# A hybrid decoder step with 32 experts: weight loads moved ahead of the read of a branch count, one more weight buffer, and the PSUM sums taken over 15 of 16 pairs

## The chip, the cores and the metric

The kernel runs on one core of one Trainium2 chip. The metric is the device time of one execution in microseconds. The kernel before was timed in three runs; the trace that is read below comes from one more, profiled execution. Engines are named as in the profile: PE is TensorE (PEld its weight loads), DVE VectorE, ACT ScalarE, POOL GpSimd, SP SyncE, which here only issues transfers.

## The reference, cut to what matters

One decoder layer is applied to 256 prompt tokens and to 8 x 8 sample tokens, 320 tokens in all, of width 1024. An adaLN projection of the conditioning gives shifts, scales and gates (`g1`, `g2`). A mixer follows (chunked gMLP and a gated linear recurrence), its output projection `w_out`, and a layer norm. Then comes the part that takes most of the time, the mixture of experts with a hidden width of 512:

```
lg = x2 @ w_rg + b_rg                       # 4 groups, top 1
le = (x2 @ w_re + b_re) of the chosen group # 8 experts, top 2
for each of the 32 experts e:
    hdn = silu(x2 @ w1[e]) * (x2 @ w3[e])   # 1024 -> 512
    acc = acc + gate[:, e] * (hdn @ w2[e])  # 512 -> 1024
x = layer_norm(ALPHA * x + (1 + g2) * acc, ln2_g, ln2_b)
```

`w1`, `w3` and `w2` have 2 MB for each expert and are read in float32: 192 MB in all. Only the tokens routed to an expert need its product.

## The kernel before, in words

**Weight buffers.** Big tiles come from two rings of 8 KB per partition (L42, `SLOTS = (8, 8)`): `slot(name, i=0)` and `slot(name, i=1)`. A ring hands on the buffer that was released first, and a tile is released after its last use in the code. The first ring holds in turn `ini`, `md` and `gx` (long-lived scratch), the adaLN weights `wada`, the halves of `w_in` and `w_out` (`wq`) and every even expert load; the second one holds the split `w_in` parts, the two `mb` tiles, `pd` and every odd expert load.

**Expert loads.** Each expert's `w1`, `w3` and `w2` come as six loads of 1 MB (tile `we`, L636). They go out on SP's queue in one fixed order: both up-projections of a pair of experts, then the down-projections of the pair before. `load_until(n)` issues them up to the n-th:

```
PIECES = [(e, i, h) for e, some in ORDER for i, h in some]
...
for e, i, h in PIECES[pieces:n]:
    w = slot("we", (128, kk, 2048 // kk), i=pieces % 2)
```

Loads 0 to 3 are issued at L639, in front of the last adaLN weights (L640) and the output projection (`out_proj`, L647). Loads up to 14 (`AHEAD = 15`) are issued at L895, and from there each pair p begins with `load_until(20 + 12 * p)` (L1137). A load waits in SP's queue for its buffer; whatever is behind it on SP waits too. At most eight transfers are under way, since each reuses the semaphore of the one eight before it.

**Routing.** `out_proj` and `norm` run over the three token tiles (128, 128 and 64 tokens); `turn_h2` (L689) transposes the normalised tokens, `logits` (L699) multiplies them with the router weights, `route` picks group and experts, `count` and `arrange` give every token its place, and `sort` (L851) gathers the tokens in order of expert into `xD`. Tiles of the pools `ab` and `mid` end here, and `xD` takes their space.

**The branch.** Each expert handles up to 24, 24 and 16 tokens of the three tiles in the main path. If some expert has more, an extra loop runs (`more_rounds`, L1010), which loads its own weights in 512-column chunks (tile `ck`, L1028, in the ring of tag `s` together with the silu tile of `swish`, L963). All engines read the count into a register:

```
n_most = nc.values_load(most[0:1, 0:1], min_val=0, max_val=NT, ...)     # L889
load_until(AHEAD)                                                      # L895
...
with tc.If(n_most > CAP):                                              # L1129
    gates_and_windows(); gates(); more_rounds()
```

With these inputs the branch is not taken. At the join, the semaphores that the body would have raised are made up for: SP waits until each of its eight transfer semaphores has reached the count of the loads issued so far, then adds what the body would have added. Consumers behind the join whose tile shares a ring with a tile of the body wait for those counts.

**Pairs of experts.** The main loop (L1136) goes over 16 pairs. `up_of(e)` (L1089) is the up-projection of one expert on PE (L959), followed by `swish` on ACT (L964) and DVE (L965); `turn_of` transposes the hidden rows of a pair (L971) and multiplies them with the gates (L974, `hT`); `downs(p - 1)` is the down-projection of the pair before (L983). Its two results are taken out of PSUM as a rounded part by ACT (L990) and the rest by DVE (L991). `places` (L946) builds the matrix that puts a pair's rows back to their tokens, and `combine` (L1000) adds them, both parts, into the five PSUM banks `pc` (L1004, L1008), which stay open over the pairs. That leaves three PSUM banks for all else.

**The last pairs.** `SUMMED = 14` pairs are summed so. After the 14th, `take()` (L1066) multiplies the sums by `g2` and adds them to the residual `xk` on DVE, and the last two pairs go another way: DVE multiplies their outputs by `g2k` when it takes them from PSUM (L987), `begin(t)` (L1044) puts the residual into the banks `pc` by an identity matmul (L1046), and `prompt_sum` and `sample_sum` (L1048, L1051) add the unsplit float32 rows. `begin_rest` (L1055) prepares the rows for the second layer norm, which ends the kernel. `g2k`, the broadcast `g2`, is a tile of its own in the pool `late`; `spread("g2", ...)` fills it at pair 2 with POOL and DVE (L511, L513).

Of the kernel before, what the change touches and what calls it, by code (L numbers as in the profile page):

```python
# [6 lines left out]
F32 = mybir.dt.float32  # L7
F32R = mybir.dt.float32r
BF16 = mybir.dt.bfloat16
# [13 lines left out]
XO = (0, 280, 560)  # L23
NP = 704
ROUNDS = 5
SUMMED = NE // 2 - 2
AHEAD = 15
SLOTS = (8, 8)
EPS = 1e-5
ALPHA = 2.0 ** 0.25  # L30
LRU_C = 8.0
# [6 lines left out]
def hymba_step(tc, I, O):  # L38
    nc = tc.nc
    with ExitStack() as ctx:  # L40
# [23 lines left out]
        eps = keep.tile([128, 1], F32, name="eps")  # L64
        mm = keep.tile([128, 2, 128], BF16, name="mm")
        before, ones = mm[:, 0, :], mm[:, 1, :]
        zz = keep.tile([1, 640], BF16, name="zz")
        zero, ones512 = zz[:, 0:128], zz[:, 128:640]
        io32 = keep.tile([128, 3, NE], F32, name="io32")
        io4 = keep.tile([128, 3, 4], F32, name="io4")  # L70
        one = keep.tile([128, 1], F32, name="one")
        lg = keep.tile([128, 3, 40], F32, name="lg")

# [46 lines left out]
        V.tensor_scalar(before, jp, 0.0, None, op0=OP.is_gt)  # L120
        V.memset(ones, 1.0)
        V.memset(zero, 0.0)
        V.memset(ones512, 1.0)
        V.memset(eps, EPS)
        V.memset(one, 1.0)
        V.memset(one[0:64], 0.0)
# [446 lines left out]
        proj_f(wy, yr_done, False, lambda: fill(2))  # L573
        early_.close()
        late = ctx.enter_context(tc.tile_pool(name="late", bufs=1, side="left"))
        g2k = late.tile([128, 2, D], F32, name="g2k")
        M = late.tile([128, 3, NE], BF16, name="M")
        sp1T = late.tile([NE, NT], F32R, name="sp1T")
        mod3 = late.tile([128, 256], F32, name="mod3")
        offs = late.tile([128, 3, NE], F32, name="offs")  # L580
        offi = late.tile([1, 3, NE], I32, name="offi")
        offf = late.tile([1, 3, NE], F32, name="offf")
        offr = late.tile([1, 3, NE], I32, name="offr")

        PT2 = [late.tile([128, 448], F32R, name=f"PT{i}") for i in range(2)]
# [1 line left out]
        h2 = scp.tile([128, 3, D], F32, name="h2")  # L587
        oh12 = scp.tile([128, 3, 2, NE], F32, name="oh12")
        io256 = late.tile([128, 256], F32, name="io256")
        mb["g2"] = (g2k[:, 0, :], g2k[0:64, 1, :])  # L590
        mb["sc2"] = (sck[:, 0, :], sck[0:64, 1, :])

        sc, sh, tmp = mod[:, 2, 0:256], mod[:, 1, 256:512], ini[:, 0:256]
# [31 lines left out]
        def load_until(n):  # L625

            nonlocal pieces
            for e, i, h in PIECES[pieces:n]:
                kk = (4, 4, 2)[i]
                w = slot("we", (128, kk, 2048 // kk), i=pieces % 2)  # L630
                pieces += 1
                src = (w1d, w3d, w2d)[i][e].rearrange("(p h k) n -> h p k n", h=2, k=kk)[h]
                parts = 2 if e == NE - 1 and i == 2 and h else 1
                step = kk // parts
                for c in range(0, kk, step):
                    nc.sync.dma_start(w[:, c:c + step], src[:, c:c + step])  # L636
                held[e, 2 * i + h] = w
# [1 line left out]
        load_until(4)  # L639
        w_g2 = load_ada2(3)  # L640
        V.memset(lg[64:128, 2, :], 0.0)
        h2T0 = mid.tile([128, D], F32, name="h2T0")
        h2T = {2: md_[:, 0:512], 0: h2T0, 1: mb["g1"][0]}
        h2T = {t: a.rearrange("p (k q) -> p k q", k=8) for t, a in h2T.items()}
        st1 = {}

        def out_proj(t, n2s=(0, 1)):  # L647
# [41 lines left out]
        def turn_h2(t, h):  # L689
            n = TW[t]  # L690
            p = bank("p2", (128, 4, 128))
            for k in range(4):
                kk = 4 * h + k
                T.transpose(p[:, k, :n], h2[:n, t, kk * 128:(kk + 1) * 128], ident[:n, :n])
            S.copy(h2T[t][:, 4 * h:4 * h + 4, :n], p[:, :, :n])

        pr = {}

        def logits(t, ks):  # L699
            n = TW[t]  # L700
            for k in ks:
                if k == 0:
                    pr[t] = bank("pr", (128, 40))
                T.matmul(pr[t][:n], h2T[t][:, k, :n], wr[:, k, :], start=(k == 0), stop=(k == 7))

        def logits_end(t):
            n = TW[t]
# [177 lines left out]
        for t in range(3):  # L885
            V.tensor_copy(offi[:, t, :], offs[0:1, t, :])
            ranks(t)
        V.tensor_reduce(most, over.rearrange("p t e -> p (t e)"), axis=AX.X, op=OP.max)
        n_most = nc.values_load(most[0:1, 0:1], min_val=0, max_val=NT,  # L889
                                skip_runtime_bounds_check_because="a count of the tokens")  # L890
        for t in range(3):
            W = XO[t] + WID[t]
            G.memset(xD[:, :, W:W + CAPS[t]], 0.0)
            G.memset(gD[:, W:W + CAPS[t]], 0.0)
        load_until(AHEAD)  # L895
        sorted_out(1)
        ada_end(3)

# [96 lines left out]
        pc = {(t, q): bank("pc") for t in range(2) for q in range(2)}  # L995
        pc[2] = bank("pc")
        for p in pc.values():
            T.matmul(p, zero, ones512, start=True, stop=False)

        def combine(yg, PT, stop=False):  # L1000
            for q in range(2):
# [7 lines left out]

        def more_rounds():  # L1010

            V.tensor_copy(offf, offs[0:1])
            with tc.For_i(0, ROUNDS, 1):
                for t in range(3):
                    V.tensor_scalar(rank[:, t, :], rank[:, t, :], -float(CAPS[t]), None, op0=OP.add)
                    V.tensor_scalar(offf[:, t, :], offf[:, t, :], float(CAPS[t]), float(WID[t]), op0=OP.add, op1=OP.min)
                    windows_of(t)
                V.tensor_copy(offr, offf)
                turn_places()
                with tc.For_i(0, NE, 2) as e:  # L1020
                    two = exs.tile([NE, 2], F32, name="two")
                    V.tensor_copy(two, ident[0:NE, bass.ds(e, 2)])
                    PT = places(select(two))
                    yg = [exs.tile([128, D], F32R, name=f"y{i}") for i in range(2)]
                    h = exs.tile([128, 512], F32, name="h")

                    def chunk(src, a, k, kk, cs):
                        c = exs.tile([128, 512], F32, name="ck", tag="s")  # L1028
                        v = src[bass.ds(e + a, 1)].rearrange("o (p k) n -> p (o k) n", k=kk)
                        nc.sync.dma_start(c, v[:, k, cs])  # L1030
                        return c

                    gT = exs.tile([128, 2, CAP], F32, name="gT")
                    for a in range(2):
                        xT, vs = window([offr[0:1, t, bass.ds(e + a, 1)] for t in range(3)], "xTm")
                        window_gates(gT, a, vs)
                        swish(a, up(lambda q, k: chunk((w1d, w3d)[q], a, k, 8, slice(0, 512)), xT), h)
                    hT = turn(h, gT)
                    for a in range(2):
                        down(a, lambda q, k: chunk(w2d, a, k, 4, slice(q * 512, q * 512 + 512)), hT, yg)  # L1040
                    combine(yg, PT)
# [93 lines left out]
        LAST = NE // 2 - 1  # L1135
        for p in range(NE // 2):  # L1136
            load_until(20 + 12 * p)  # L1137
            if p < LAST:
                select_of(p)
            if p == 0:  # L1140
                fetch(1)
                gates_and_windows()
            up_of(2 * p)
            fetch(2 * p + 2)
            if p == 2:
                spread("g2", 2, (range(4), slice(256, 512)))
            if p == 5:
                row1 = slot("row1", (1, 2048), i=1)
                G.dma_start(row1[:, 0:1024], I["ln1_g"])
                G.dma_start(row1[:, 1024:2048], I["ln1_b"])  # L1150
                ln1 = slot("ln1", (128, 2048))
                G.partition_broadcast(ln1, row1, channels=128)
            if 6 <= p < 9:
                whiten[p - 6]()
                residual(p - 6)
            if p >= 2 and p < LAST:
                combine(ys.pop(p - 2), PTs.pop(p - 2))
            if 0 < p < LAST:
                places_of(p)
            fetch(2 * p + 3)  # L1160
            if p == LAST:
                downs(p - 1)
                begin(0)
                begin(1)
                for t in range(2):
                    for q in range(2):
                        prompt_sum(t, q, ys[p - 1], PTs[p - 1], False)
                sample_sum(ys[p - 1], PTs[p - 1], False)
            second = up_of(2 * p + 1)
            if p == 0:  # L1170
                gates()
                gates_of(0, first)
                gates_of(1, second)
                turn_places()
                places_of(0)
            if p == LAST - 2:
                f1 = slot("f1", (128, 128), i=1)
                fold = f1.rearrange("p (a n) -> p a n", a=2)
                sv = exs.tile([128, 2], F32, name="sv")
                f2 = slot("f2")  # L1180
                g2s, G2s, B2s, xs = (f2[:, 512 * i:512 * i + 512] for i in range(4))
                lrow = slot("lrow", (1, 2048), i=1)
                G.dma_start(lrow[:, 0:1024], I["ln2_g"])  # L1183
                G.dma_start(lrow[:, 1024:2048], I["ln2_b"])
                lbc = slot("lbc", (128, 2048))
                G.partition_broadcast(lbc, lrow, channels=128)
            if p == LAST - 1:
                begin_rest()
            if p and p < LAST:
                downs(p - 1)  # L1190
            turn_of(p)
            if p == LAST - 1:
                combine(ys.pop(p - 1), PTs.pop(p - 1), True)
                select_of(LAST)
                places_of(LAST)
                take()
        S.activation(sv[:, 0:1], eps, AF.Sqrt)
        down_of(NE - 2)
        S.activation(sv[:, 0:1], eps, AF.Sqrt)
# [81 lines left out]
```

## Time and profile before

| | us |
|---|---|
| runs of the kernel before | 691.79, 687.49, 690.62 (median 690.62) |
| profiled execution, its own time | 687.08 |
| its span | 685.3 |
| PE busy (2762 matmuls) | 600.3 (88% of the span) |
| DVE busy | 276.0 (40%) |
| ACT busy | 127.9 (19%) |
| POOL busy | 51.7 (8%) |

HBM reads are 241.49 MB, 355 GB/s over the span. The own time is 1.8 us longer than the span, which begins with the first and ends with the last record of an engine.

The page cuts the span into 40 slices of 17.1 us. In the rows of groups and of the timeline stand: start or line, engine, operation, written tile <- read tiles, partitions x elements, count; what a bracket or the last column holds is the idle time of the engine just before and what ended it. In a row of waits the numbers are the total, the count of waits, and the longest. A row of windows gives, for a stretch, the busy time of PE, PEld, DVE, ACT and POOL with their counts, then the granted PE clock, the DMA share and GB/s. A PE that is busy need not be the bound: its matmuls are pipelined.

### The profile page before, as it was taken

What the parts mean: (1) busy time and instruction counts of PE and PEld (TensorE: products, weight loads), DVE (VectorE), ACT (ScalarE), POOL (GpSimd) and SP (SyncE); (2) the same over time, 40 slices, a digit from 0 to 9 for tenths busy, and PEclk for the clock granted to TensorE, in tenths of its full rate; (3) what the DMA queues carried; (4) which work ended last, traced back from release to release, by engine and by line L of the source; (5) the groups of instructions that cost most, each with busy time, mean ns of one, the idle gap of its engine ahead of it and who ended that gap; (6) DMA issues with size and microseconds to landing.
All of it is one profiled execution on the core that took longest, in us unless ns stands there. A gap on an engine that the chain in (4) does not pass through costs nothing.

```text
span 685.3 us, 7676 instructions
## 1 busy us (share of the span) xinstructions
PE 600.3 (88%) x2762; PEld 272.7 (40%) x2762; DVE 276.0 (40%) x748; ACT 127.9 (19%) x219; POOL 51.7 (8%) x81
## 2 busy tenths in 40 slices
PE   5599999999974999998989898897989989897982
PEld 1396688356621343332323333232332323233320
DVE  1399484966522243233134243322323132225226
ACT  0255651111201011111012111101111010112121
POOL 2031415300010000000020000000000000100002
PEclk9989999999795999999999999999999999998997
DMA  8997678831298999999999999999999999999902
GB/s 336 383 324 268 237 250 314 307 127 63 105 424 328 426 427 427 426 427 427 427 426 427 427 427 426 427 425 428 425 428 426 427 427 427 425 427 427 413 23 77
DMA packets 42493, 243.57 MB, mean 355 GB/s; under 512 B 5630, under 2 KB 6374, under 8 KB 15954
## 3 DMA queue, kind: packets, MB, share of 16 engines
q1 hardware_dynamic: 41650, 242.58, 86.9%
q0 software_dynamic: 800, 0.45, 0.3%
q8 instruction: 23, 0.38, 0.2%
q14 instruction: 20, 0.16, 0.1%
HBM read 241.49 MB, written 1.52 MB: 355 GB/s over the span
## 4 chain that ended last, share of the span: by engine, by line
DMA 46%; PE 18%; DVE 2%; ACT 1%; issue 0%; SPq 0%; ACTq 0%
DMA we<-in_w 46%; PE p L959 9%; PE p L983 5%; PE pc L1004 1%; PE pc L1049 1%; PE pc L1008 1%; PE pc L1046 1%; PE ph L971 0%; DVE y L991 0%; PE pc L1053 0%; PE pr L949 0%; PE pgd L909 0%; DVE xk L1249 0%; DVE h L965 0%; DVE f L987 0%
## 5 line engine op out<-in xcount | busy, mean ns | idle before, releaser
L959 PE MATMUL p<-we,xT 128*64 128x512 f32 x1024 | 244.0, 605 | 27.2 <-DMA we<-in_w 25.6
L959 PEld LDWEIGHTS p<-we,xT 128*64 128x64 f32 x1024 | 75.1, 138 | 174.5 <-issue 126.9
L983 PE MATMUL p<-we,hT 128*64 128x512 f32 x512 | 116.8, 597 | 7.2 <-DMA we<-in_w 6.4
L965 DVE TENSOR_TENSOR h<-p,s 64x512 f32<-64x512 f32 x32 | 22.2, 694 | 147.4 <-ACT s L964 146.7
L964 ACT ACTIVATE s<-p 64x512 f32<-64x512 f32 x32 | 18.9, 589 | 305.0 <-PE p L959 279.5
L983 PEld LDWEIGHTS p<-we,hT 128*64 128x64 f32 x512 | 35.4, 137 | 85.3 <-issue 63.2
L991 DVE TENSOR_TENSOR y<-p,y 64x512 fp32r<-64x512 f32 x56 | 38.6, 689 | 70.3 <-ACT y L990 70.3
L931 DVE COPY xT<-xD 128x192 f32 (+1 forms) x96 | 23.8, 248 | 93.0 <-PE p L959 77.7
L990 ACT CAST y<-p 64x512 fp32r<-64x512 f32 x56 | 32.4, 579 | 87.4 <-PE p L983 66.3
L1004 PE MATMUL pc<-y,PT 128*128 128x512 f32 x112 | 31.7, 425 | 4.1 <-ACT y L990 4.1
L177 PE MATMUL ada<-wada,md 128*32 128x512 f32 (+1 forms) x256 | 28.7, 560 | 4.3 <-DMA wada<-in_w_ada 2.7
L1004 PEld LDWEIGHTS pc<-y,PT 128*128 128x128 f32 x112 | 21.0, 197 | 19.3 <-issue 10.5
L354 PE MATMUL pf<-hH,whi 128*128 128x320 f32 x64 | 20.6, 322 | 0.0
L354 PE MATMUL pf<-hL,whi 128*128 128x320 f32 x64 | 19.8, 309 | 0.0
L354 PE MATMUL pf<-hH,wlo 128*128 128x320 f32 x64 | 19.7, 308 | 0.0
L1183 POOL DMA_DIRECT2D lrow<-in_ln_g x1 | 0.5, 500 | 229.9 <-PE p L983 229.9
L1008 PE MATMUL pc<-y,PT 128*128 128x512 f32 x56 | 15.6, 402 | 0.0
L295 DVE TENSOR_TENSOR wlo<-wq,whi 128x1024 fp32r<-128x1024 f32 x12 | 15.3, 1336 | 0.0
L971 PEld LDWEIGHTS ph<-ident,h 128*128 128x128 f32 x64 | 9.1, 210 | 14.0 <-issue 9.2
L657 PE MATMUL po<-wq,uT 128*128 128x512 f32 x32 | 14.7, 601 | 0.0
L909 PE MATMUL pgd<-pd 128*128 128x256 f32 (+1 forms) x6 | 2.6, 548 | 13.5 <-DVE h L965 13.5
L858 PE MATMUL px<-pd,h 128*128 128x256 f32 (+1 forms) x48 | 14.2, 465 | 0.2 <-DVE pd L776 0.2
(336 smaller groups left out, 601.3 us busy)
## 6 DMA issues: line engine op xcount, KB each, us to landing
we<-in_w SPq DMA_DIRECT2D x191, 1024.0 KB, 19.6
wada<-in_w_ada SPq DMA_DIRECT2D x24, 1024.0 KB, 5.2
wq<-in_w_in SPq DMA_DIRECT2D x8, 1024.0 KB, 4.9
wq<-in_w_out SPq DMA_DIRECT2D x4, 1024.0 KB, 5.0
xk<-in_x_prompt SPq DMA_DIRECT2D x1, 1024.0 KB
we<-in_w SPq DMA_DIRECT2D x2, 512.0 KB
out_y_prompt<-xk SPq DMA_DIRECT2D x4, 256.0 KB, 2.1
xk<-in_x_sample SPq DMA_DIRECT2D x1, 256.0 KB
```

The costliest lines, as they stand in the source:

```text
L177: T.matmul(ada_p[g][32 * j:32 * j + 32, :], cT[:, k, :], wj, start=(k == 0), stop=(k == 7))
L295: eng.tensor_tensor(lo[:, c:c + 2], w[:, c:c + 2], hi[:, c:c + 2].bitcast(F32), op=OP.subtract)
L354: T.matmul(p, w[k // 4][part][:, k % 4, f * 128:(f + 1) * 128], x[:, k, :], start=(i == 0 and k == 0), stop=(i == 2 and k == 7))
L931: V.tensor_copy(xT[:, :, BASE[t]:BASE[t] + CAPS[t]], xD[:, :, XO[t]:XO[t] + WID[t] + CAPS[t]][:, :, bass.ds(v, CAPS[t])])
L959: T.matmul(p[64 * q:64 * q + 64, :], xT[:, k, :], w(q, k), start=(k == 0), stop=(k == 7))
L964: S.activation(s[64:128, :], p[0:64, :], AF.Silu)
L965: V.tensor_tensor(h[64 * a:64 * a + 64, :], p[64:128, :], s[64:128, :], op=OP.mult)
L983: T.matmul(p[q], hT[:, k, sl], w(q, k), start=(k == 0), stop=(k == 3))
L990: S.copy(yg[0][sl, cs], p[q])
L991: V.tensor_tensor(yg[1][sl, cs], p[q], yg[0][sl, cs].bitcast(F32), op=OP.subtract)
L1004: T.matmul(pc[t, q], PT[:, TOFF[t]:TOFF[t] + 128], yg[i][:, H[q]], start=False, stop=stop and i == 1)
L1008: T.matmul(pc[2], PT[:, cs], yg[i][:, H[q]], start=False, stop=False)
```

## The change

- `load_until(AHEAD)` stands directly in front of the read of the branch count instead of behind it and behind POOL's memsets.
- The branch body's tile `ck` gets a ring of its own.
- The first ring has nine buffers (`SLOTS = (9, 8)`). Space for it comes from: `g2k`, which is no longer a tile of its own but takes a buffer of the first ring from pair 12 on, where `spread("g2", ...)` now stands; `h2T0`, since the transposed tokens now go into `abT`, whose columns `out_proj` has read by then; the row of 512 ones, since the zeroing matmuls of `pc` go in halves of 256 columns over `mm`; `offf`, since the branch now works in `offs`; and `io32` and `io4`, which move from the pool `keep` to `ab`.
- `SUMMED` is 15: the pair before the last is combined like the others, and `take()` comes after it. In the last round of the loop the order on PE becomes up(30), combine(13), places(15), downs(14), combine(14), up(31), begin(0), turn(15), begin(1), downs(15), where the numbers of up are experts and the others pairs. Before, the last two rounds had, from downs(13) on, turn(14), combine(13), places(15), up(30), downs(14), begin(0), begin(1), the plain sums of pair 14, up(31), turn(15), downs(15).

```diff
-SUMMED = NE // 2 - 2
+SUMMED = NE // 2 - 1
 AHEAD = 15
-SLOTS = (8, 8)
+SLOTS = (9, 8)
...
-        zz = keep.tile([1, 640], BF16, name="zz")
-        zero, ones512 = zz[:, 0:128], zz[:, 128:640]
-        io32 = keep.tile([128, 3, NE], F32, name="io32")
-        io4 = keep.tile([128, 3, 4], F32, name="io4")
+        zero = keep.tile([1, 128], BF16, name="zero")
+        io32 = ab.tile([128, 3, NE], F32, name="io32")
+        io4 = ab.tile([128, 3, 4], F32, name="io4")
...
-        g2k = late.tile([128, 2, D], F32, name="g2k")
...
-        offf = late.tile([1, 3, NE], F32, name="offf")
...
-        h2T0 = mid.tile([128, D], F32, name="h2T0")
-        h2T = {2: md_[:, 0:512], 0: h2T0, 1: mb["g1"][0]}
-        h2T = {t: a.rearrange("p (k q) -> p k q", k=8) for t, a in h2T.items()}
...
-            S.copy(h2T[t][:, 4 * h:4 * h + 4, :n], p[:, :, :n])
+            S.copy(abT[h][:, :, TOFF[t]:TOFF[t] + n], p[:, :, :n])
...
+        load_until(AHEAD)
         n_most = nc.values_load(most[0:1, 0:1], min_val=0, max_val=NT,
                                 skip_runtime_bounds_check_because="a count of the tokens")
...
-        load_until(AHEAD)
         sorted_out(1)
         ada_end(3)
...
         for p in pc.values():
-            T.matmul(p, zero, ones512, start=True, stop=False)
+            for q in range(2):
+                T.matmul(p[:, 256 * q:256 * q + 256], zero, mm[0:1].rearrange("p a n -> p (a n)"), start=(q == 0), stop=False)
...
-            V.tensor_copy(offf, offs[0:1])
+            offf = offs[0:1]
...
-                        c = exs.tile([128, 512], F32, name="ck", tag="s")
+                        c = exs.tile([128, 512], F32, name="ck")
...
         for p in range(NE // 2):
             load_until(20 + 12 * p)
-            if p < LAST:
-                select_of(p)
+            select_of(p)
...
             up_of(2 * p)
             fetch(2 * p + 2)
-            if p == 2:
+            if p == LAST - 3:
+                g2k = slot("g2k").rearrange("p (a n) -> p a n", a=2)
+                mb["g2"] = (g2k[:, 0, :], g2k[0:64, 1, :])
                 spread("g2", 2, (range(4), slice(256, 512)))
...
-            if p >= 2 and p < LAST:
+            if p >= 2:
                 combine(ys.pop(p - 2), PTs.pop(p - 2))
+            if p == LAST:
+                places_of(p)
             if 0 < p < LAST:
                 places_of(p)
             fetch(2 * p + 3)
             if p == LAST:
                 downs(p - 1)
-                begin(0)
-                begin(1)
-                for t in range(2):
-                    for q in range(2):
-                        prompt_sum(t, q, ys[p - 1], PTs[p - 1], False)
-                sample_sum(ys[p - 1], PTs[p - 1], False)
+            if p == LAST:
+                combine(ys.pop(p - 1), PTs.pop(p - 1), True)
+                take()
             second = up_of(2 * p + 1)
...
             if p and p < LAST:
                 downs(p - 1)
+            if p == LAST:
+                begin(0)
             turn_of(p)
-            if p == LAST - 1:
-                combine(ys.pop(p - 1), PTs.pop(p - 1), True)
-                select_of(LAST)
-                places_of(LAST)
-                take()
+            if p == LAST:
+                begin(1)
```

More of the change, by code (lines that the diff above doesn't have):

```diff
@@ L122, in hymba_step @@
         V.memset(zero, 0.0)
-        V.memset(ones512, 1.0)
         V.memset(eps, EPS)
@@ L589, in hymba_step @@
         io256 = late.tile([128, 256], F32, name="io256")
-        mb["g2"] = (g2k[:, 0, :], g2k[0:64, 1, :])
         mb["sc2"] = (sck[:, 0, :], sck[0:64, 1, :])
@@ L703, in logits @@
                     pr[t] = bank("pr", (128, 40))
-                T.matmul(pr[t][:n], h2T[t][:, k, :n], wr[:, k, :], start=(k == 0), stop=(k == 7))
+                T.matmul(pr[t][:n], abT[k // 4][:, k % 4, TOFF[t]:TOFF[t] + n], wr[:, k, :], start=(k == 0), stop=(k == 7))
         def logits_end(t):
```

## The prediction

> **What bounds the kernel now.** I read the slices of the page and its chain first, then the chain in order of time, then the windows between 150 and 220 us, then who waited for whom.
>
> ```profile
> span 685.3 us, 7676 instructions
> ...
> GB/s 336 383 324 268 237 250 314 307 127 63 105 424 328 426 427 427 426 427 427 427 426 427 427 427 426 427 425 428 425 428 426 427 427 427 425 427 427 413 23 77
> ...
> DMA 46%; PE 18%; DVE 2%; ACT 1%; issue 0%; SPq 0%; ACTq 0%
> ```
>
> From slice 14 on the core moves 427 GB/s without a break, and the chain that ends last is nearly all expert loads (DMA) and, in the last 55 us, PE. Two rows of that chain, one pair of experts apart, give PE's own pace, and one row of the DMA issues gives that of the loads:
>
> ```profile
> 243.29 0.68 PE ph L971 x4
> 250.99 2.06 PE pc L1004 x8
> 253.04 0.92 PE pc L1008 x4
> 268.19 0.68 PE ph L971 x4
> ```
>
> ```profile
> we<-in_w SPq DMA_DIRECT2D x191, 1024.0 KB, 19.6
> ```
>
> PE needs 268.19 - 243.29 = 24.9 us for a pair. A load lands 19.6 us after its issue with eight under way, so 2.45 us each, and a pair of experts has twelve: 29.4 us. The loads set the pace, and whoever starts the stream earlier ends it earlier. So the question is what holds the stream before slice 14.
>
> ```profile
> 170.00:180.00 10.00, 9.83 (x35) 8.48 (x35) 4.99 (x24) 1.76 (x3) 0.00 (x0) 0.69 0.00 0
> 180.00:190.00 10.00, 8.46 (x31) 4.55 (x32) 7.11 (x34) 4.15 (x7) 0.76 (x6) 0.83 0.66 242
> 210.00:220.00 10.00, 4.29 (x12) 2.23 (x12) 4.14 (x16) 2.60 (x6) 0.00 (x0) 0.50 0.67 259
> 240.00:640.00 400.00, 363.82 (x1560) 135.81 (x1558) 124.94 (x333) 57.03 (x95) 6.77 (x6) 0.99 1.01 427
> ```
>
> The last two columns are the DMA share and GB/s: nothing at all moves from 170 to 180, and there is a second hole after 210.
>
> ```profile
> SPq L889 <- DVE most L888: 24.4, 1, 24.4
> SPq L636 <- DMA we<-in_w: 342.9, 167, 3.0
> SPq L636 <- PE p L959: 15.0, 11, 4.5
> ```
>
> ```profile
> ACT s L964 <- SPq L1129: 24.7, 1, 24.7
> ```
>
> ```profile
> L1129 SPq EVENT_SEMAPHORE  x8: 17/17/17, 208.5 to 213.7; - x8
> L1129 SPq COMPARE_BRANCH  x1: 50/50/50, 193.8 to 193.8; - x1
> ```
>
> The first hole is SP's 24.4 us in front of the read of the branch count. Only then does it issue loads 4 to 14 (I count the 1 MB expert loads from 0; 0 to 3 went out at 120). At the join of the branch not taken SP waits on eight semaphores, one for each DMA lane, and leaves at 213.7, when its newest load has landed. That is the second hole. ACT's silu tile shares its ring with the tile that the branch body loads, so ACT waits out the same join for 24.7 us.
>
> ```profile
> 156.95 0.37 SPq L200 DMA_DIRECT2D wada<-in_w_ada  x1
> 160.37 3.66 PE L177 MATMUL ada<-wada,md 128*32 128x256 f32 x64
> 174.55 0.58 ACT L845 COPY xD<-px 128x512 f32<-128x512 f32 x1 [3.30 <-PE px L858]
> 182.36 36.79 SPq L636 DMA_DIRECT2D we<-in_w  x20
> 183.61 0.41 DVE L188 SCALAR_TENSOR_TENSOR mod<-ada,md 128x256 f32<-128x256 f32 x1
> 185.44 15.65 PE L959 MATMUL p<-we,xT 128*64 128x512 f32 x64 [1.54 <-DVEq L1129]
> ```
>
> ```profile
> 201.01 0.70 PE L909 MATMUL pgd<-pd 128*128 128x256 f32 x2
> 215.20 1.95 PE L909 MATMUL pgd<-pd 128*128 128x256 f32 x4 [13.49 <-DVE h L965]
> 220.02 9.04 PE L959 MATMUL p<-we,xT 128*64 128x512 f32 x32
> ```
>
> PE does the first two experts (185.44, 64 matmuls in 15.65 us, so 7.8 us each), then idles 13.5 us because ACT stands still, and begins the third expert at 220.02.
>
> **The change, part by part.**
>
> *Loads 4 to 14 ahead of the count.* SP goes past one register read; POOL's and the other engines' queues are not passed. What counts is when the buffers of these eleven loads come free. I followed the rings through the code: each hands on the buffer that was released first. With nine instead of eight buffers in the first ring every later tile of that ring takes the buffer one step older. Before, the last adaLN load waits for the third w_out tile and goes at 156.95; after, that buffer goes to load 4, so load 4 goes at 156.95. Load 6 gets the fourth w_out tile, free when PE starts the adaLN matmuls at 160.37; loads 8 to 14 of that ring get the four adaLN tiles, free one after the other until 160.37 + 3.66 = 164.0 (before, load 14 needed the `md` tile, which DVE leaves at 184.0). The odd loads come from the other ring, where the w_in halves and the two `mb` tiles are free by then; moving the turned `h2` from `mb` into `abT` helps that. Load 6 at 160.4 finds two loads of 2.45 us queued, so the stream does not run dry. Before, these eleven took from 182.36 to 213.7 = 31.3 us; after, 156.95 + 31.3 = 188.3. SP reads the count at the same time as the others, and leaves the join at 188.3 instead of 213.7.
>
> Load 15 is next. It takes the buffer of load 1, which PE frees halfway through the first expert: 185.44 + 15.65/4 = 189.4. So the unbroken stream starts at 189.4 instead of 213.7, **24.3 us earlier**. If some of the eleven wait longer, the start slips by that much: 3 us late would cost 1.9 us. It can't start before 189.4 unless PE does.
>
> Can PE give buffers back fast enough? With no stall after 201.01, the gates, places and turns that took 220.02 - 215.20 = 4.8 us, behind the 0.7 of the gate matmuls at 201.01, put the third expert at 206.5. Load 25 needs the buffer of load 9, free halfway through it, at 210.2; the stream wants it at 189.4 + 10 x 2.45 = 213.9. The margin is 3.7 us, and it grows by 29.4 - 24.9 = 4.5 us a pair. I cost this at nothing; the cover is that margin.
>
> *Own ring for the branch tile.* ACT no longer waits for the join: 24.7 us of wait go, PE's 13.5 us with it. On the path this only makes room for the line above.
>
> *The 15th pair in the PSUM sums.* This is the tail, where PE sets the end:
>
> ```profile
> 621.73 4.19 PE L1004 MATMUL pc<-y,PT 128*128 128x512 f32 x8 [4.09 <-ACT y L990]
> 627.58 7.09 PE L959 MATMUL p<-we,xT 128*64 128x512 f32 x32
> 634.49 7.04 PE L983 MATMUL p<-we,hT 128*64 128x512 f32 x32
> 641.46 3.70 PE L1046 MATMUL pc<-xk,ident 128*128 128x512 f32 x8
> 645.00 3.60 PE L1049 MATMUL pc<-yf,PT 128*128 128x512 f32 x8
> 648.52 1.08 PE L1053 MATMUL pc<-yf,PT 128*64 128x512 f32 x4
> 649.43 7.04 PE L959 MATMUL p<-we,xT 128*64 128x512 f32 x32
> 657.95 0.75 PE L971 MATMUL ph<-ident,h 128*128 128x128 f32 x4 [1.48 <-DVE h L965]
> 659.48 7.09 PE L983 MATMUL p<-we,hT 128*64 128x512 f32 x32 [0.78 <-DVE hT L974]
> ```
>
> ```profile
> 621.11 1.41 DVE L991 TENSOR_TENSOR y<-p,y 64x512 fp32r<-64x512 f32 x2 [0.65 <-ACT y L990]
> ```
>
> Before, PE does combine(13) from 621.73, up(30) from 627.58, downs(14) from 634.49, then begin 3.54, prompt_sum 3.52, sample_sum 0.91, up(31) from 649.43, and the last downs from 659.48. After, in the old times: up(30) comes first; it needs a PSUM bank, and DVE frees one at 621.11 + 0.69 = 621.8. It ends at 628.7 (6.9). combine(13) no longer waits: 2.06 + 0.92 + 0.34 for places, 632.0. downs(14) 7.0: 639.0. combine(14) waits for the last expert's outputs, about 0.6 + 0.7 us for their first half by the DVE row and its 0.65 us of waiting: 640.4, and takes 2.98 plus about 0.4 for the second half: 643.8. up(31): 650.8. begin(0), 1.8, lies in the 1.48 us in which PE waits for swish; begin(1), 1.8, in the 0.78 us for hT. 650.8 + 1.8 + 0.75 + 1.8 = 655.2 against 659.48: **4.3 us less**. take() moves onto DVE between combine(14) and swish(31):
>
> ```profile
> L1070 DVE TENSOR_TENSOR pc<-pc,g2k x4: 687/693/693, 628.3 to 632.3; 128x512 f32<-128x512 f32 x4
> ```
>
> Eight such, 5.5 us, under up(31)'s 7.0. Without that cover swish(31) and begin(0) wait, at most 5.5 us, and the gain of the tail turns to a loss of 1.2. The other end is the whole of begin and the sums, 8 us, less combine(14)'s 3.0: a gain of 5.0.
>
> *g2 at pair 12 instead of 2.*
>
> ```profile
> L513 DVE STREAM_SHUFFLE g2k<-mod x8: 425/430/435, 253.8 to 256.9; 32x256 f32<-32x256 f32 x8
> ```
>
> The tile now takes a slot whose buffer PE frees at the end of up(25). Eight shuffles, 3.4 us, stand in DVE's queue until then, and behind them places(12), the windows of expert 27 and swish(25), some 2.2 us. PE meanwhile has downs(11), 6.9 us, so I cost it at nothing; without cover up to 5.6 us, in a stage where PE has 4.5 us to spare in every pair. From there on the first ring has eight buffers again, as before.
>
> *Small ones*, at nothing: twice as many zeroing matmuls (in PE's idle time before 185.44); `io32` now lies where `xD` comes, so ACT's first `xD` copy may wait about 1 us for DVE's read of it, and ACT idles 3.30 us before the next such copy at 174.55; the dropped `offf` copy is in the branch.
>
> **Sum.** 685.3 (span) - 24.3 - 4.3 = 656.7, and 687.08 - 685.3 = 1.8 outside the span: 658.5 for an execution like the profiled one. That one, 687.08, lies 3.5 under the median of the runs, 690.62; I carry half of that, 1.8: **660 us**. For the range: 0 or 3.5 of that offset, -0.7 to +5.5 on the tail, 0 to 3 for a late stream: 656 to 667 for this case alone, and a little below for what nobody sees.
>
> **The rivals.**
>
> 1. *PE's buffers pace the stream.* For it: SP already waited for PE 11 times, 15.0 us. Then the stream follows PE, which starts the third expert 220.0 - 206.5 = 13.5 earlier, not 24.3: 658.5 + 10.8 + 1.8 = 671. Against it: the 3.7 us of margin.
>
> 2. *The branch's code is fetched behind the loads.* Now up to (188.3 - 182.4)/2.45 = 2.4 loads are under way when PE, ACT and DVE branch; before, their loads only began. A fetch that waits for all of them costs 5.9 us, and there are two jumps, into the empty branch and out of it: 11.8 on PE's start and so on load 15, 672. SP's own branch at 193.8 under full load speaks neither way, since it then waits for the landing of loads in any case; its jump out, at 213.7, was followed by loads at once. [...]
>
> 3. *The loads don't go ahead*: a buffer among the eleven comes free only behind the branch (as `md` did at 184.0 for the last one). If that held for load 4, the stream would be where it was, and only the tail's 4.3 us would stay: 690.62 - 4.3 = 686, within 1%.
>
> 4. *Slower: the routing chain runs beside full DMA.* Between 156.95 and 185.44 the core moves next to nothing today; after, 427 GB/s go into SBUF beside the same DVE, ACT and PE work. If that work takes longer, experts and load 15 start later. The price is the stretch of 28.5 us times the slowing; from a factor of 2.0 it eats all 28.6 us of gain; at 2.3, 37 us: 690.62 + 8 = 699. Against it: DVE's 128x512 or 64x512 operations show 0.69 us in the tail rows at full DMA, no more than the 0.41 for half the elements at 183.61 would suggest.
>
> **How the numbers follow.** Forecast 0.74, rival 1 0.11, rival 2 0.07, rival 3 0.05, rival 4 0.03. Faster by over 1% (a bound that is about what a measurement here can tell): 0.92; within 1%: 0.05; slower: 0.03. The range goes from 654 to 671: it takes in rival 1 and leaves out about 0.15 above and a little below.
>
> **What would show it.** GB/s near 427 from about 157 to 186; SP's last semaphore at the join near 188; no wait of ACT for SP; third expert near 206.5; the stream unbroken from about 190 and ended near 627; combine(13) behind up(30) with no 4 us of idle time before it; plain sums (L1049) for the last pair alone. Wrong if load 4 goes out much after 157, if SP waits for PE in long stretches between 190 and 300, or if PE's first expert starts after 187.

## The result, and the profile after

The changed kernel takes 668.62 us (median of four runs, 668.5 to 671.64), the kernel before, on the same chip, 691.2 (four runs, 687.49 to 691.92). The ratio is 0.969, interval 0.965 to 0.974. That is 22.6 us less, where 30.6 had been forecast (690.62 to 660); the time lies inside the stated range of 654 to 671, and outside the 656 to 667 that the prediction gave "for this case alone". The profiled execution has a span of 666.5 us and a time of its own of 668.5. Line numbers after the change are 5 to 8 lower: the read of the count is L882, the branch L1122, the loads L631, the up-projection L951, the down-projection L975, their outputs L982 and L983.

The page of the changed kernel, and its DMA issues:

```profile
span 666.5 us, 7641 instructions
...
GB/s 326 382 327 357 261 192 327 320 109 268 421 259 423 420 421 420 420 421 421 422 419 421 421 421 421 422 418 422 419 424 420 421 420 421 420 422 418 419 49 79
...
DMA 42%; PE 26%; DVE 2%; ACT 1%; issue 0%; SPq 0%
```

```profile
we<-in_w SPq DMA_DIRECT2D x191, 1024.0 KB, 19.8
```

```profile
160.00:170.00 10.00, 8.88 (x99) 6.12 (x98) 8.31 (x25) 1.47 (x3) 0.00 (x0) 0.98 0.99 417
170.00:180.00 10.00, 9.84 (x36) 8.57 (x35) 5.07 (x25) 1.76 (x3) 0.00 (x0) 0.68 1.02 423
180.00:190.00 10.00, 8.46 (x36) 4.95 (x37) 7.17 (x31) 4.15 (x7) 0.76 (x6) 0.84 0.70 286
190.00:200.00 10.00, 10.00 (x50) 3.30 (x48) 4.91 (x20) 0.59 (x1) 0.00 (x0) 0.99 0.75 287
...
240.00:600.00 360.00, 326.46 (x1408) 121.22 (x1406) 106.35 (x296) 47.91 (x80) 8.78 (x10) 1.00 1.01 421
```

Two things are to be seen. The empty stretch from 160 to 180 is full, and the hole behind the branch has shrunk to one around 190. But the plateau is lower: 421 GB/s where there were 427, and 19.8 us where a load took 19.6. Over some 440 us that is 6 us, and nothing in the prediction has it.

SP's own waits, its expert loads ahead of the count, its semaphores at the join, its first loads behind the join, and PE's first experts:

```profile
SPq L631 <- PE p L951: 20.7, 12, 4.8
...
SPq L882 <- DVE most L880: 12.9, 1, 12.9
```

```profile
157.58 11.77 SPq L631 DMA_DIRECT2D we<-in_w  x11
```

```profile
L1122 SPq EVENT_SEMAPHORE  x8: 17/17/17, 188.5 to 189.2; - x8
```

```profile
191.49 7.67 SPq L631 DMA_DIRECT2D we<-in_w  x6
```

```profile
185.95 15.79 PE L951 MATMUL p<-we,xT 128*64 128x512 f32 x64 [1.52 <-DVEq L1122]
...
205.34 7.09 PE L951 MATMUL p<-we,xT 128*64 128x512 f32 x32
```

SP has all eleven loads out 12.9 us before the count is there. It leaves the join at 189.2 (before: 213.7) and issues load 15 at 191.5 (before: 213.8). PE goes from the second expert into the third at 205.34 (before: 220.02), and ACT's wait for SP is gone from the list.

The tail on PE, from the same load as the old 595.41 on, and two windows in it:

```profile
578.97 3.65 PE L951 MATMUL p<-we,xT 128*64 128x512 f32 x14 [1.31 <-DMA we<-in_w]
...
605.60 8.78 PE L951 MATMUL p<-we,xT 128*64 128x512 f32 x32 [4.13 <-DVE y L983]
614.32 2.12 PE L997 MATMUL pc<-y,PT 128*128 128x512 f32 x8
...
617.63 7.09 PE L975 MATMUL p<-we,hT 128*64 128x512 f32 x32
625.39 0.50 PE L997 MATMUL pc<-y,PT 128*128 128x512 f32 x1 [0.68 <-ACT y L982]
...
629.28 7.09 PE L951 MATMUL p<-we,xT 128*64 128x512 f32 x32
636.29 1.98 PE L1039 MATMUL pc<-xk,ident 128*128 128x512 f32 x4
...
640.39 7.09 PE L975 MATMUL p<-we,hT 128*64 128x512 f32 x32
```

```profile
604.00:607.00 3.00, 1.40 (x6) 0.53 (x8) 1.67 (x4) 1.74 (x3) 0.00 (x0) 0.93 1.00 418
607.00:610.00 3.00, 3.00 (x10) 0.87 (x8) 1.42 (x3) 0.00 (x0) 0.00 (x0) 0.50 1.02 426
```

up(30) waits for a PSUM bank, 4.13 us, as the prediction had it (621.8 in the old times, 26.4 us behind the load; here 26.6). But then it runs at a granted clock of 0.50 and takes 8.78 us where 6.9 were counted. Before, the same idle time came ahead of combine(13), a shorter piece.

### The profile page after: what moved, and what is told of

Its sections match the earlier page's. It is cut to its first block, busy times and chain, and to the rows that moved or that the text cites. A ratio compares the mean times of both kernels' runs of the same rounds, so it can differ in the third digit from the quotient of the medians.

```text
span 666.5 us, 7641 instructions
## 1 busy us (share of the span) xinstructions
PE 593.7 (89%) x2767; PEld 270.7 (41%) x2767; DVE 274.3 (41%) x747; ACT 128.2 (19%) x219; POOL 52.5 (8%) x81
## 3 DMA queue, kind: packets, MB, share of 16 engines
HBM read 241.49 MB, written 1.52 MB: 365 GB/s over the span
## 4 chain that ended last, share of the span: by engine, by line
DMA 42%; PE 26%; DVE 2%; ACT 1%; issue 0%; SPq 0%
DMA we<-in_w 42%; PE p L951 15%; PE p L975 6%; PE pc L997 2%; PE pc L1001 1%; PE pc L1039 1%; PE ph L963 0%; DVE y L983 0%; PE pr L941 0%; ACT y L982 0%; PE pgd L901 0%; DVE xk L1241 0%; DVE f L979 0%; DVE xk L1238 0%; ACT f L1054 0%
## 5 line engine op out<-in xcount | busy, mean ns | idle before, releaser
L951 PE MATMUL p<-we,xT 128*64 128x512 f32 x1024 | 242.5, 603 | 30.8 <-DMA we<-in_w 25.0
L951 PEld LDWEIGHTS p<-we,xT 128*64 128x64 f32 x1024 | 74.4, 138 | 176.6 <-issue 126.4
L975 PE MATMUL p<-we,hT 128*64 128x512 f32 x512 | 117.1, 596 | 8.4 <-DMA we<-in_w 6.6
L983 DVE TENSOR_TENSOR y<-p,y 64x512 fp32r<-64x512 f32 x60 | 41.3, 688 | 79.7 <-ACT y L982 79.7
L975 PEld LDWEIGHTS p<-we,hT 128*64 128x64 f32 x512 | 35.7, 137 | 86.6 <-issue 57.7
L982 ACT CAST y<-p 64x512 fp32r<-64x512 f32 x60 | 34.8, 580 | 98.9 <-PE p L975 74.5
L175 PE MATMUL ada<-wada,md 128*32 128x512 f32 (+1 forms) x256 | 28.5, 558 | 4.8 <-DMA wada<-in_w_ada 3.1
L352 PE MATMUL pf<-hL,whi 128*128 128x320 f32 x64 | 19.8, 309 | 0.0
L509 POOL PARTITION_BROADCAST g2k<-mod x4 | 1.8, 548 | 197.2 <-PE p L951 197.2
L649 PE MATMUL po<-wq,ga 128*128 128x512 f32 x32 | 14.4, 592 | 0.0
L293 DVE TENSOR_TENSOR wlo<-wq,whi 128x1024 fp32r<-128x1024 f32 x12 | 13.9, 1218 | 0.0
## 6 DMA issues: line engine op xcount, KB each, us to landing
we<-in_w SPq DMA_DIRECT2D x191, 1024.0 KB, 19.8
```

The costliest lines, as they stand in the source:

```text
L175: T.matmul(ada_p[g][32 * j:32 * j + 32, :], cT[:, k, :], wj, start=(k == 0), stop=(k == 7))
L352: T.matmul(p, w[k // 4][part][:, k % 4, f * 128:(f + 1) * 128], x[:, k, :], start=(i == 0 and k == 0), stop=(i == 2 and k == 7))
L649: T.matmul(p, abT[k // 4][:, k % 4, ts], wo[n2][k // 4][:, k % 4, :], start=(k == 0), stop=(k == 7))
L951: T.matmul(p[64 * q:64 * q + 64, :], xT[:, k, :], w(q, k), start=(k == 0), stop=(k == 7))
L975: T.matmul(p[q], hT[:, k, sl], w(q, k), start=(k == 0), stop=(k == 3))
L982: S.copy(yg[0][sl, cs], p[q])
```

## The experiments

Executions of one kernel differ by up to 6.3 us here (no_ahead, 690.05 to 696.35). The spans and PE's first expert show where: the profiled kernel before starts it at 185.44, another execution of it at 190.37, and the rest is 499.9 and 500.2 us. So the kernels are also compared by the time from PE's first expert matmul to the end of the span, which leaves that part out. It arises in the first 57 us: the adaLN loads behind the third pair of `w_in` loads go out at 53.20 in the one and at 57.50 in the other execution, between 53.09 and 57.50 in all profiled executions, and from there to PE's first expert all need 131.9 to 133.3 us. What delays them there was not settled.

| kernel | span | first expert | from there to the end | GB/s, 300 to 560 |
|---|---|---|---|---|
| before, profiled first | 685.3 | 185.44 | 499.9 | 427 |
| before, again (b0) | 690.6 | 190.37 | 500.2 | 427 |
| after | 666.5 | 185.95 | 480.6 | 421 |
| after, again (a0) | 670.6 | 189.24 | 481.4 | 421 |
| loads_only | 665.3 | 187.89 | 477.4 | 427 |
| no_ahead | 690.8 | 186.43 | 504.4 | 421 |
| shift64 | 692.4 | 185.72 | 506.7 | 421 |
| shift128 | 696.7 | 190.25 | 506.5 | 421 |
| shift256 | 688.8 | 189.09 | 499.7 | 427 |
| aligned | 660.4 | 185.53 | 474.9 | 427 |
| aligned_shared | 661.4 | 186.76 | 474.6 | 427 |
| aligned_old_tail | 667.7 | 189.43 | 478.3 | 427 |
| aligned_rest | 662.1 | 189.66 | 472.4 | 427 |
| eight_rest | 659.5 | 186.95 | 472.6 | 427 |

**Whose is the slower pace?** One execution each, on one chip, of the kernel before and of the changed one, both unchanged.

> The kernel before, unchanged, on the chip of this batch, for the pace of the loads. If the slower pace of the loads in the changed kernel (19.83 us for eight against 19.6, 421 against 427 GB/s) belongs to the chip or the execution and not to the change, some profiles of the unchanged kernel show 421 GB/s too, and then its span is near 690. If the change itself slows the loads (nine buffers, other addresses), every profile of the unchanged kernel shows 427 and the span is near 685.

> The changed kernel again, on the same chip as the unchanged one. If the pace of the loads belongs to the chip, both have the same GB/s here, and the difference of the spans is 22 to 25 us. If the change slows the loads, this one has 421 where the unchanged one has 427.

The windows of b0 and of a0 between 300 and 560 us:

```profile
300.00:560.00 260.00, 234.49 (x1001) 86.04 (x999) 75.96 (x202) 34.35 (x56) 3.50 (x3) 1.00 1.01 427
```

```profile
300.00:560.00 260.00, 229.43 (x975) 84.54 (x971) 77.20 (x212) 34.62 (x56) 5.28 (x7) 1.00 1.01 421
```

427 and 421 on the same chip: the pace belongs to the kernel. That b0's span, expected near 685, is 690.6 at 427 GB/s shows that its longer time comes from elsewhere, as said above. The spans differ by 20.0, and from the first expert to the end by 18.8.

**The loads ahead and nothing else.**

```diff
+        load_until(AHEAD)
         n_most = nc.values_load(most[0:1, 0:1], min_val=0, max_val=NT,
...
-        load_until(AHEAD)
         sorted_out(1)
```

> The kernel before with the loads up to 14 in front of the read of the count, and nothing else: eight buffers, the shared ring, 14 summed pairs. My theory: the stream's start is all that counts; load 4 goes when the adaLN matmuls start (160 us instead of 157), load 14 when the md tile is free (184), the join ends near 189 to 192, load 15 goes near 192. That gives 20 to 22 us of the 22.6, about 670 where the changed kernel has 668.6. Rival: the ninth buffer is what lets the loads go ahead; then load 14, held by md behind the branch, or the shared ring, holds ACT and PE again, and the gain is under 10 us.

667.5 us, ratio 0.968 (0.963 to 0.972). SP's semaphores at the join, PE's first experts:

```profile
L1129 SPq EVENT_SEMAPHORE  x8: 17/17/17, 192.8 to 193.9; - x8
```

```profile
187.89 14.61 PE L959 MATMUL p<-we,xT 128*64 128x512 f32 x64 [1.52 <-DMA we<-in_w]
```

477.4 us behind the first expert, 22.5 to 22.8 less than before. One moved line gives all that the whole change gives, and as a time it can't be told from it: in the changed kernel what the rest gains (the tail) and what it loses (the pace of the loads) leave no net gain. The rival is out.

**Everything but the loads ahead.**

```diff
-        load_until(AHEAD)
         n_most = nc.values_load(most[0:1, 0:1], min_val=0, max_val=NT,
...
+        load_until(AHEAD)
         sorted_out(1)
         ada_end(3)
```

> The changed kernel with the loads back behind the read of the count (ninth buffer, own ring and 15 summed pairs stay). My theory: ACT and PE no longer stop at the join, PE begins the third expert near 206, but load 15 still goes at about 213.8, PE soon waits for it, and the end moves by the tail alone: 2 to 3 us faster than before, about 688. Rival: PE's 13.5 us of standing still were the loss; then this one is 13 us faster or more, under 678.

693.3 us, ratio 1.005 (1.003 to 1.007): 0.5% slower, where both theories had it faster. The join, and PE's third and fourth expert:

```profile
L1122 SPq EVENT_SEMAPHORE  x8: 17/17/17, 209.6 to 215.3; - x8
```

```profile
208.20 7.09 PE L951 MATMUL p<-we,xT 128*64 128x512 f32 x32
...
221.70 3.22 PE L951 MATMUL p<-we,xT 128*64 128x512 f32 x13 [1.64 <-DMA we<-in_w]
```

PE does begin the third expert 12 us earlier than before, at 208.20, and gets nothing for it: at 221.70 it waits for the loads, whose stream starts at 215.3 as ever. The 13.5 us of standing still cost nothing. What makes it slower is the pace, 421 GB/s: by the runs below the pace costs 5.7 to 6.5 us and the new tail gives some 2.4 back, 3.3 to 4.1, where 504.4 is 4.5 more than 499.9.

**Where the buffers start.** The first pool lost 1280 - 256 bytes of `zz`, 384 of `io32` and 64 of `io4` (48, rounded up) per partition, 1472 in all. The weight buffers, 8192 bytes each and one behind the other, began at byte 33792 of each partition, 66 x 512; now they begin at 32320, 63 x 512 + 64. One small tile moved out of that pool brings them to 32256 = 63 x 512:

```diff
-            eg = keep.tile([128, 3, 4], F32, name="eg")
+            eg = late.tile([128, 3, 4], F32, name="eg")
```

> The changed kernel with one 48-byte tile (eg) moved from the first pool to a later one, so that the weight buffers start at byte 32256 of each partition, a multiple of 512, as they did before (33792), instead of 32320, which is 64 past such a multiple. Theory: the start of the buffers sets the pace of the loads; then 427 GB/s from 200 on instead of 421, and with 177 loads of 1 MB (186 MB) left the stream ends 186/0.421 - 186/0.427 = 6 us earlier: about 662.5. Rival: the ninth buffer (other addresses in general, more rows) slows the loads; then 421 GB/s and 668.6 stay.

The other way round, the kernel before with a tile of 64, 128 or 256 bytes more in that pool, so that its buffers start at 33856, 33920 or 34048:

```diff
+        pad = keep.tile([128, 16], F32, name="pad")
+        nc.vector.memset(pad, 0.0)
```

> The kernel before with 64 bytes more in the first pool, so that its sixteen buffers start at 33856, 64 past a multiple of 512; nothing else changes. Theory (start of the buffers): 421 GB/s, and 6 us slower than before, about 696. Rival (the ninth buffer): 427 GB/s and no difference.

> The kernel before with its buffers 128 bytes further, at 33920: a multiple of 128 and not of 256. If 256 bytes is the unit, 421 GB/s; if 128 is enough, 427.

> The same with 256 bytes: the buffers start at 34048, a multiple of 256 and not of 512. If 256 bytes is the unit, 427 GB/s; if it is 512, 421.

The windows from 300 to 560 us of aligned, shift64, shift128 and shift256, in this order:

```profile
300.00:560.00 260.00, 234.22 (x1003) 86.61 (x1000) 78.11 (x217) 34.07 (x55) 5.29 (x7) 1.00 1.01 427
```

```profile
300.00:560.00 260.00, 231.79 (x981) 86.55 (x983) 73.93 (x199) 33.51 (x54) 3.50 (x3) 1.00 1.01 421
```

```profile
300.00:560.00 260.00, 231.69 (x983) 86.80 (x985) 73.45 (x195) 32.70 (x54) 3.50 (x3) 1.00 1.01 421
```

```profile
300.00:560.00 260.00, 233.59 (x996) 85.53 (x994) 74.95 (x200) 34.09 (x55) 3.50 (x3) 1.00 1.01 427
```

Shifting the old kernel by 64 bytes makes it 0.9% slower (ratio 1.009, 1.006 to 1.012), 506.7 us behind the first expert instead of 499.9; 128 bytes do the same; 256 bytes do nothing (one execution each). Aligning the changed kernel gives 474.9 instead of 480.6 to 481.4, 5.7 to 6.5 us. Its ratio is 0.964 (0.962 to 0.967). The rival, the ninth buffer as such, is out: with nine buffers that start at 32256, a multiple of 256, the pace was 427. The runs' medians say less than the traces, since the spread ahead of the first expert lies on top: 665.85 came where 662.5 was expected.

**The own ring.** The aligned version with `tag="s"` back on `ck`.

> The aligned version with the branch tile back in the ring of the silu tile. My theory: with the loads ahead SP leaves the join near 188 to 192, before ACT has its first silu to do (PE ends the first expert 8 us after it starts), so the own ring is worth nothing: from the first expert's first matmul to the end 474 to 476 us, as in the aligned version (474.9). Rival: ACT and the join still meet, and the time is 2 us longer or more.

474.6, one execution: worth nothing that shows, as expected, once the loads are ahead. A difference under some 2 us isn't resolved here: up(30), behind the same 4.1 to 4.2 us of PE idle time, takes 8.5 us in aligned and 10.0 in this execution.

**The tail.** The aligned version with the summing and the order of the last pairs as before.

> The aligned version with the tail of the kernel before (14 summed pairs, two plain ones, the old order). It tells what the 15th summed pair is worth by itself. By the traces 2.5 us: 477.4 from the first expert to the end against 474.9, and about 0.4% slower than the aligned version; the prediction had 4.3. Rival: the tail is hidden behind the loads; then 474.9 stays.

478.3, ratio 0.967 (0.965 to 0.970) against 0.964: the new tail is worth 3.4 us by this pair. But half of that is the granted clock in this one execution, whose last down-projection, with the same short gap ahead of it as before the change, takes 8.78 us instead of 7.09:

```profile
639.89 8.78 PE L975 MATMUL p<-we,hT 128*64 128x512 f32 x32 [0.79 <-DVE hT L966]
```

```profile
640.00:643.00 3.00, 3.00 (x10) 0.89 (x12) 0.00 (x0) 0.00 (x0) 0.00 (x0) 0.57 0.00 0
```

From the load at 595.41 and 578.97 to the end, the traces before and after have 89.9 and 87.5, 2.4, and loads_only and aligned differ by 2.5. It is not hidden, and it is less than 4.3.

**The idle time in the tail.** ACT's eight copies of `begin_rest` stand ahead of the outputs of downs(13). Moved behind combine(13), into pair 15:

```diff
-            if p == LAST - 1:
-                begin_rest()
...
             if p == LAST:
+                begin_rest()
                 places_of(p)
```

> The aligned version with begin_rest moved from pair 14 to pair 15, behind combine(13): ACT's eight copies then no longer stand in front of the outputs of downs(13). In the changed kernel PE waits 4.1 us there for a PSUM bank, and its clock falls, so that up(30) takes 8.8 us instead of 7.0. Theory: both go, but the loads then bind (e30's last load lands 29.5 us after the one that the chain leaves at), so of 5.9 us some 2 to 3 remain: 2 to 3 us faster than aligned, about 660. Rival: the wait is hidden behind the loads anyway; then no difference.

PE's up(30) in that version:

```profile
599.03 1.05 PE L951 MATMUL p<-we,xT 128*64 128x512 f32 x2
601.39 3.65 PE L951 MATMUL p<-we,xT 128*64 128x512 f32 x16 [1.31 <-DMA we<-in_w]
606.27 3.65 PE L951 MATMUL p<-we,xT 128*64 128x512 f32 x14 [1.23 <-DMA we<-in_w]
```

The wait for the bank and the slow clock are gone (granted 1.00 from 597 to 615; 16 of the matmuls take 3.65 us, as at 571.95, a pair earlier), and the loads bind instead: 472.4 against 474.9, 2.5 us. The ratio, 0.959 (0.955 to 0.963), is the lowest of all, though its interval overlaps that of aligned.

**The ninth buffer.** The last version with eight buffers, and `g2k` a tile of its own again.

> The aligned version with begin_rest at pair 15, but with eight buffers in the first ring and g2k as a tile of its own again (buffers from 32256 on). It tells what the ninth buffer is worth. My theory: nothing that counts; load 4 waits for the adaLN matmuls (3 us later) and load 14 for md (184), but load 15 waits for PE's first expert in any case: 472 to 475 us from the first expert's first matmul to the end (472.4 with nine), and a time within 0.5% of the version with nine. Rival: the ninth buffer carries the gain; then 5 us more or worse.

472.6 us, ratio 0.963 (0.960 to 0.967): the ninth buffer is worth nothing.

```profile
L1123 SPq EVENT_SEMAPHORE  x8: 17/17/17, 191.9 to 192.4; - x8
```

## Why the prediction was right, and where it was off

**The mechanism held.** The loads ahead carry the gain: 22.5 to 22.8 us by themselves, of 24.3 forecast. Load 4 went at 157.6 as counted, and the join ended at 189.2 (188.3). Of ACT's own ring the forecast said that on the path it "only makes room"; no_ahead and aligned_shared show that it gives nothing, with the loads behind the count or ahead of it. `g2` at pair 12 cost nothing that shows, as counted: DVE waits 7.5 us there for its buffer, and eight_rest, where `g2k` has a tile of its own, takes the same time (472.6 against 472.4).

**The step that failed: the price of a load.** "A load lands 19.6 us after its issue with eight under way, so 2.45 us each" was read before the change and kept for after it. The first pool's small edits were costed "at nothing" by their instructions; that they move the start of all weight buffers was not asked. It cost 5.7 to 6.5 us, most of what was missing. Six starts were run: 427 GB/s from 32256, 33792 and 34048, multiples of 256, and 421 from 32320, 33856 and 33920, which lie 64, 64 and 128 bytes past one; 427 / 421 = 1.4%. What was moved is the side written. Where in the copy the time goes was not measured.

**Mis-sized: the start of load 15.** The prediction had it 4.0 us behind PE's first expert matmul (a quarter of 15.65); it came 5.5 behind it (191.49 - 185.95). PE's clock is low just there (0.50 from 187 to 190), so the first quarter of the two experts is slower than their mean. Three us at half the clock are 1.5 of the 1.6 us. The trace before has the same, as these rows of the kernel after and before show, but the prediction took a quarter of the whole:

```profile
187.00:190.00 3.00, 2.98 (x10) 0.69 (x8) 2.30 (x11) 1.79 (x4) 0.00 (x0) 0.50 0.06 22
```

```profile
187.00:190.00 3.00, 3.00 (x10) 1.18 (x8) 2.48 (x13) 1.80 (x4) 0.00 (x0) 0.52 1.01 412
```

Meanwhile the DMA engines ran dry, 286 and 287 GB/s around 190, which is what is left of the hole.

**Mis-sized: the tail.** 4.3 forecast, 2.4 to 2.5 measured at like clocks. The order and the waits came as worked out, up(30)'s bank within 0.2 us, but up(30) was given 6.9 us and took 8.78: behind the 4.13 us in which PE had stood still, the granted clock was 0.50 in the window from 607 to 610. The same low clock also came behind shorter gaps, 1.52 us ahead of the first expert (0.50) and, in aligned_old_tail, 1.48 and 0.79 us (0.57); before the change, 1.48 and 0.78 us at that place left it at 1.00 (655 to 659.4, 659.5 to 666). How long an idle time lowers it was not shown. The rows before the change showed the price already: combine(13) took 4.19 + 1.58 us instead of 2.98, at 0.50 from 621.7 to 625.

```profile
625.73 1.58 PE L1008 MATMUL pc<-y,PT 128*128 128x512 f32 x4
```

take() lay under up(31), as counted.

These three make 5.7 to 6.5, 1.6 and 1.8 to 1.9, together 9.1 to 10.0. From the first expert to the end, 656.7 - 185.44 = 471.3 had been forecast and 480.6 was measured, 9.3 more. aligned_rest and eight_rest reach 472.4 and 472.6, but with an edit that the forecast did not have.

**The range.** Its terms do not add up to 656 to 667: 658.5 with 0 or 3.5, -0.7 to +5.5 and 0 to 3 gives 657.8 to 670.5. None of these terms is the price of a load, which took most of the miss. The wider range, 654 to 671, was drawn to take in rival 1, so that the time falls into it is in part luck. By the time alone, 668.6, rival 1 at 671 is nearer than the forecast; only the traces and the runs tell them apart.

**The rivals.** PE's buffers do not pace the stream: SP waited for PE 20.7 us in 12 waits (before 15.0 in 11), and behind 200 no slice of the page falls under 418 GB/s while the stream lasts. The chain does follow PE further than before, to 297.57 instead of 278.77, so PE's share of it rises from 18 to 26%; but the load that it passes to there lands 19.81 us after its issue, as the others do, so the queue was full all the same. And with the loads at 427 GB/s the time falls as the price of a load says (aligned). The branch's code is not late behind the loads: PE idles 1.52 us ahead of its first expert (before 1.54), with loads under way. That each jump waits 5.9 us for its code was the author's estimate; no run shows such a wait. The loads do go ahead. The routing chain is not slowed by them: from 157.58, load 4, to 185.95 it takes 28.4 us (before 28.5, from 156.95 to 185.44).

**The offset.** Half of the 3.5 us between the profiled execution and the median of before was carried over. That part is the spread ahead of the first expert, and the changed kernel's profiled execution, 668.5, lies at its median. So the median came 8.6 us above the forecast of 660, and the profiled execution 10.0 above its own, 658.5.

## What to carry to other kernels

Where the loads set the pace, look for the instruction that their queue waits at for no need of their own (here a register read in front of a branch not taken), and move the loads in front of it; freeing the engines that stood still beside it was worth nothing by itself here. Before memory is rearranged, compute where the big buffers of the stream will start, and look up or measure the pace of the loads for that start: here it was 427 GB/s on a multiple of 256 bytes (32256, 33792, 34048) and 421 at 64 or 128 bytes past one (32320, 33856, 33920). When an edit's gain is taken from a piece behind a PE idle time of some 4 us, look in the windows for the clock that was granted there, count the piece at that clock (here 0.50 behind 4.13 us, and 8.78 us for 6.9), or remove the idle time first.

## What the runs showed of the hardware that was not expected

Transfers of 1 MB into rows of 8 KB, eight under way, ran at 427 GB/s when the sixteen buffers started at byte 33792 or 34048 of each partition (b0, shift256), multiples of 256, and at 421 when they started at 33856 or 33920, 64 or 128 bytes past 33792 (shift64, shift128), with everything else alike.
